# The sums of quarters for Strassen's products: from two engines to one, and lower in the scheduler's order

## The chip, the cores and the metric

The kernel runs on one core of a Trainium2 chip. Its engines work side by side, each through its own list of instructions in order: TensorE (PE) multiplies matrices, VectorE (DVE), ScalarE (ACT) and GpSimd (POOL) work elementwise, and the queue of SyncE (SP) issues the DMA transfers. The metric is the time of one execution in microseconds (us).

## The reference

The reference is two layers of a transformer-like backbone over 512 latent tokens and 256 context tokens of width 1024: a pooling mixer in layer 0, attention in layer 1, and behind each a squared-ReLU MLP with 4096 hidden units.

```
h = h + g1 * mixer(modulate(rms_norm(h)))
m = modulate(rms_norm(h))
h = h + g2 * (square(relu(m @ w1)) @ w2)
```

The change lies in the two MLPs. In layer 0 it also computes the context tokens, in layer 1 the latent tokens alone.

## The kernel before, in words

All activations lie transposed in SBUF: features on the partitions, tokens along the row. To keep float32 precision each operand of a product is split into a high part (ACT copies it, line 84, 379 or 461) and a residual (DVE subtracts, line 85, 381 or 463), and PE makes three products: high by high, high by residual, residual by high. The helper for the split is `hilo`. A weight `w` is thus a DMA into a staging tile `raw` (two buffers, so the DMA for the next one but one waits for the residual to be made), an ACT copy and a DVE subtraction.

An MLP (`mlp`) walks through 16 chunks of 256 hidden units. For each chunk `m1_chunk` (products on line 369) makes `m @ w1` into PSUM; `m1_done` applies ReLU and square (ACT lines 377, 379 and 380, DVE line 381) and leaves `act`. Then `m2_chunk` (products on line 486) makes the product with `w2` for the chunk before, in eight blocks `dt` of 128 output features; after each, DVE adds it to `h_lat` and `h_ctx` (`add_gated`, line 346). The PSUM tiles `mm` have two buffers, `aux` four, so a block waits until an older one has been read.

From chunk 5 of layer 0 and chunk 4 of layer 1 on, the latent part of `m @ w1` is computed by Strassen's scheme: seven products of quarters instead of eight (line 435). For that, five sums or differences of quarters of `m` are prepared once per layer, in `strassen_inputs`. A quarter of `m` is 128 partitions by 1024 numbers, and has a high part and a residual (`m_m_hi`, `m_m_lo`). `total` makes one of them: `s` from the two high parts, on DVE; `e` from the two residuals, on POOL (both line 392); `s + e`, on DVE (line 393); and the split of it by `hilo`. Three of the results are the tiles `xs`; the other two overwrite a quarter of `m` itself. The temporary tiles `s` and `e` are named `op` in layer 0 and `mc` in layer 1.

These five sums are issued in steps beside the first calls of `m2_chunk` (the parameter `side`): in layer 0 from about 132 us on, in layer 1 from about 954 us. In the same stretches DVE also serves the weights and the outputs of the chunks, and in layer 0 the products of layer 1's conditioning vector (`ada1_block`: lines 215 and 217, split into the tiles `ada0` and `ada1`, and PE's products on line 225).

Behind its first part, which is ordered by hand, the order on each engine is made by a list scheduler at build time: among instructions that are ready by its own estimate it takes the one with the lowest rank, and the rank is the place in the program. The order is then fixed: on the chip an engine never overtakes. In the Strassen chunks POOL makes sums of quarters of the weights (line 424, tiles `sc`), with or without this change.

Of the kernel before, what the change touches and what calls it, by code (L numbers as in the profile page):

```python
# [8 lines left out]
F32 = mybir.dt.float32  # L9
F32R = mybir.dt.float32r  # L10
AF = mybir.ActivationFunctionType
ALU = mybir.AluOpType
# [27 lines left out]
ADA_1 = (0, 2, 4, 5, 6, 1, 7, 3, 8, 9, 10, 11)  # L40

STRASSEN_FROM = (5, 4)


@with_exitstack
def dit_block_kernel(ctx: ExitStack, tc: tile.TileContext, xT, cols, adab, adaw, w1, w2, wqkv, wo,
                     poolw, gvec, rope, edge, eye, out):
    nc = tc.nc
    act, dve, pool, pe = nc.scalar, nc.vector, nc.gpsimd, nc.tensor
# [22 lines left out]
    def new(p, shape, dt, tag, bufs=None):  # L72
        uid[0] += 1
        kw = {"bufs": bufs} if bufs else {}
        return p.tile(shape, dt, tag=tag, name=f"{tag}{uid[0]}", **kw)
# [7 lines left out]
    def hilo(hi, lo, src, lo_eng=dve):  # L83
        act.activation(hi, src, AF.Copy)  # L84
        lo_eng.tensor_tensor(lo, src, hi.bitcast(F32), op=ALU.subtract)  # L85
# [297 lines left out]
    def strassen_inputs(m, xs, tmp, cuts):  # L383


        def quarter(i, j):
            return [m[0][x][:, 4 * i : 4 * i + 4, 256 * j : 256 * j + 256] for x in range(2)]

        def total(dst, a, b, op):
            s, e = (new(tmp[0], [P, 4, 256], F32, tmp[1]) for _ in range(2))  # L390
            for o, x, eng in ((s, 0, dve), (e, 1, pool)):
                eng.tensor_tensor(o, a[x].bitcast(F32), b[x].bitcast(F32), op=op)  # L392
            dve.tensor_tensor(s, s, e, op=ALU.add)  # L393
            hilo(dst[0], dst[1], s)

        b11, b12, b21, b22 = (quarter(i, j) for i in range(2) for j in range(2))
        b7, b6, b1 = ([t[:, x] for x in range(2)] for t in xs)
        sums = ((b7, b21, b22, ALU.add), (b6, b11, b12, ALU.add), (b1, b11, b22, ALU.add),
                (b12, b12, b22, ALU.subtract), (b21, b21, b11, ALU.subtract))

        def steps(todo):
            for x in todo:
                total(*x)
                yield
        return (b22, b12, b21, b11, b7, b6, b1), [steps(sums[i:j]) for i, j in zip((0,) + cuts, cuts + (5,))]
# [152 lines left out]
    for g, win in enumerate(WINDOWS):  # L558
# [6 lines left out]
        for e in range(3):  # L565

            todo = [(bands[:, g, e, 1:], cur[:, PAD + 1 : 3 * PAD + P], PAD + 1)]
            if e:
                o = PAD if e == 1 else P
# [12 lines left out]
    for k in range(0, KT, 2):  # L582
        for s, c0, n in segs:
# [4 lines left out]
            dst, src = turned[s][:, : n // P, k * P : k * P + 256], ps.rearrange("p (i c) -> p i c", c=256)  # L588
# [76 lines left out]
    for dt in range(8):  # L665
        if dt % 2 == 0:
            b = (4, 3, 5, 6)[dt // 2]
# [144 lines left out]
    def strassen0(m):  # L812
# [9 lines left out]
        def op():  # L822
# [9 lines left out]
            return tile_of  # L832
        return STRASSEN_FROM[0], strassen_inputs(m, xs, (opp, "op"), (0, 1, 3)), lambda: new(rawp, [P, 2, 1024], F32, "pair"), op

# [238 lines left out]
    def strassen1(m):  # L1073
# [4 lines left out]
        xs = [xsp.tile([P, 2, 4, 256], F32R, tag=f"xs{i}", name=f"xs{i}") for i in range(3)]  # L1078
        return STRASSEN_FROM[1], strassen_inputs(m, xs, (mc, "mc"), (1, 3)), lambda: new(fin, [P, 2, 1024], F32, "fin"), op

# [95 lines left out]
```

## Time and profile before

| | us |
|---|---|
| median of three runs | 1305.57 (1305.48 to 1306.43) |
| the profiled execution | 1306.94 |
| its span, first to last instruction | 1305.2 |
| PE busy in it | 1249.4 |
| DVE busy | 1036.6 |
| ACT busy | 578.4 |
| POOL busy | 325.1 |

The profile shows one execution. A line of its timeline has the start, the length, the engine, the line of the kernel, the operation, the tile written and the tiles read, how many neighbours were merged, and in brackets how long the engine had been idle before it and what ended that. PE's granted clock is 1.00 at 2.4 GHz and 0.50 at 1.2 GHz; a stretch's mean lies between.

### The profile page before, as it was taken

What the parts mean: (1) busy time and instruction counts of PE and PEld (TensorE: products, weight loads), DVE (VectorE), ACT (ScalarE), POOL (GpSimd) and SP (SyncE); (2) the same over time, 40 slices, a digit from 0 to 9 for tenths busy, and PEclk for the clock granted to TensorE, in tenths of its full rate; (3) what the DMA queues carried; (4) which work ended last, traced back from release to release, by engine and by line L of the source; (5) the groups of instructions that cost most, each with busy time, mean ns of one, the idle gap of its engine ahead of it and who ended that gap; (6) DMA issues with size and microseconds to landing.
All of it is one profiled execution on the core that took longest, in us unless ns stands there. A gap on an engine that the chain in (4) does not pass through costs nothing. (4 is left out here: it accounts for less than half of the span.)

```text
span 1305.2 us, 20489 instructions
## 1 busy us (share of the span) xinstructions
PE 1249.4 (96%) x8150; PEld 1109.4 (85%) x8150; DVE 1036.6 (79%) x1671; ACT 578.4 (44%) x954; POOL 325.1 (25%) x223
## 2 busy tenths in 40 slices
PE   7999989999999999999988999999979999999997
PEld 6567868899999999999878799998967899989896
DVE  6564998788989888866888387879899788898976
ACT  5454513444444444443343154445553535444443
POOL 0000320122131322230135122211054244343411
PEclk8999989999999999999999999999989999999998
DMA  9766314333433333301111020111214323322211
GB/s 351 270 241 226 113 54 157 113 130 114 145 109 135 114 129 130 130 33 52 46 57 66 33 66 34 65 33 65 98 33 133 114 95 111 98 97 98 66 33 65
DMA packets 41313, 138.68 MB, mean 106 GB/s; under 512 B 4736, under 2 KB 8064, under 8 KB 41088
## 3 DMA queue, kind: packets, MB, share of 16 engines
q1 hardware_dynamic: 41216, 137.36, 29.9%
q8 instruction: 64, 1.05, 0.3%
q14 instruction: 33, 0.27, 0.1%
HBM read 135.25 MB, written 2.10 MB: 105 GB/s over the span
## 5 line engine op out<-in xcount | busy, mean ns | idle before, releaser
L486 PE MATMUL mm<-act,w 128*128 128x512 f32 (+1 forms) x1224 | 244.4, 352 | 11.9 <-DVE act L381 6.3
L486 PE MATMUL aux<-act,w 128*128 128x512 f32 (+1 forms) x1224 | 240.0, 347 | 3.2 <-DVE h_lat L346 3.1
L486 PEld LDWEIGHTS mm<-act,w 128*128 128x128 f32 x1224 | 199.5, 193 | 44.8 <-DVE act L381 6.6
L486 PEld LDWEIGHTS aux<-act,w 128*128 128x128 f32 x1224 | 196.3, 190 | 32.8 <-DVE h_lat L346 3.9
L84 ACT ACTIVATE w<-raw 128x1024 fp32r<-128x1024 f32 x106 | 110.2, 1054 | 138.2 <-PE aux L486 89.0
L85 DVE TENSOR_TENSOR w<-raw,w 128x1024 fp32r<-128x1024 f32 x87 | 112.4, 1305 | 33.7 <-ACT w L84 33.1
L346 DVE SCALAR_TENSOR_TENSOR h_lat<-aux,mod,h_lat 128x512 f32<-128x512 f32 (+1 forms) x204 | 125.4, 629 | 16.3 <-PE aux L486 14.6
L424 POOL TENSOR_TENSOR sc<-pair 128x512 f32<-128x512 f32 x55 | 76.8, 1405 | 221.4 <-DVE op L430 88.8
L424 POOL TENSOR_TENSOR sc<-fin 128x512 f32<-128x512 f32 x60 | 90.5, 1523 | 154.0 <-DVE r L444 87.4
L346 DVE SCALAR_TENSOR_TENSOR h_lat<-mm,mod,h_lat 128x512 f32<-128x512 f32 (+1 forms) x140 | 96.6, 698 | 7.6 <-PE mm L486 6.7
L369 PE MATMUL mm<-m_m_hi,w 128*128 128x512 f32 (+1 forms) x320 | 92.5, 351 | 1.1 <-ACT m_m_hi L84 1.1
L856 PE MATMUL aux<-w,a_m_hi 128*128 128x256 f32 (+1 forms) x384 | 87.5, 323 | 0.0
L217 DVE SCALAR_TENSOR_TENSOR mc<-raw,s_f,mc 128x512 f32<-128x512 f32 x112 | 84.8, 777 | 2.5 <-DMA raw<-in_dram 1.7
L85 POOL TENSOR_TENSOR w<-raw,w 128x1024 fp32r<-128x1024 f32 x19 | 47.2, 2497 | 100.1 <-ACT w L84 99.7
L435 PE MATMUL mm<-m_m_hi,mc 128*128 128x256 f32 x384 | 71.0, 283 | 0.0
L856 PEld LDWEIGHTS aux<-w,a_m_hi 128*128 128x128 f32 x384 | 64.4, 193 | 4.9
L369 PEld LDWEIGHTS mm<-m_m_hi,w 128*128 128x128 f32 x320 | 56.1, 189 | 11.1 <-ACT m_m_hi L84 1.3
L455 PE MATMUL aux<-m_c,w 128*128 128x256 f32 x528 | 65.2, 283 | 0.0
L455 PEld LDWEIGHTS aux<-m_c,w 128*128 128x128 f32 x528 | 64.2, 192 | 0.0
L463 DVE TENSOR_TENSOR act<-r,act 128x512 fp32r<-128x512 f32 x46 | 48.4, 1052 | 19.8 <-ACT r L462 19.7
L856 PE MATMUL aux<-w,a_m_lo 128*128 128x256 f32 (+1 forms) x192 | 61.7, 321 | 0.0
L435 PEld LDWEIGHTS mm<-m_m_hi,mc 128*128 128x128 f32 x384 | 60.7, 192 | 0.5
(245 smaller groups left out, 2612.1 us busy)
## 6 DMA issues: line engine op xcount, KB each, us to landing
raw<-in_dram SPq DMA_DIRECT2D x157, 512.0 KB, 3.3
praw<-in_dram SPq DMA_DIRECT2D x34, 512.0 KB, 8.1
fin<-in_dram SPq DMA_DIRECT2D x24, 512.0 KB, 4.1
pair<-in_dram SPq DMA_DIRECT2D x22, 512.0 KB, 4.2
block<-in_dram SPq DMA_DIRECT2D x8, 512.0 KB, 6.2
h_lat<-in_dram SPq DMA_DIRECT2D x4, 512.0 KB, 6.4
w<-in_dram SPq DMA_DIRECT2D x4, 512.0 KB, 10.7
out_dram<-fin SPq DMA_DIRECT2D x8, 256.0 KB, 2.5
```

The costliest lines, as they stand in the source:

```text
L84: act.activation(hi, src, AF.Copy)
L85: lo_eng.tensor_tensor(lo, src, hi.bitcast(F32), op=ALU.subtract)
L217: dve.scalar_tensor_tensor(acc[:, s], w, scal, acc[:, s], op0=ALU.mult, op1=ALU.add)
L346: dve.scalar_tensor_tensor(h, ps, gate[:, dt, s : s + 1], h, op0=ALU.mult, op1=ALU.add)
L369: pe.matmul(ps[:, c0 : c0 + cn], lhs, ms(m, ax, k, c0, cn), start=k + wx + ax == 0, stop=k == KT - 1 and wx == 1)
L424: pool.tensor_tensor(t, x, y, op=how)
L435: pe.matmul(places[n], w[:, wx, k * P : k * P + P], inputs[n][ax][:, k], start=k + wx + ax == 0, stop=k == 3 and wx == 1)
L455: pe.matmul(pc[:, t * 256 : t * 256 + 256], ws[k // 4][:, wx, k % 4 * P : k % 4 * P + P], ms(m, ax, k, SEQ, CTX), start=k + wx + ax == 0, ...
L463: dve.tensor_tensor(lo, r, hi.bitcast(F32), op=ALU.subtract)
L486: pe.matmul(ps, lhs, a[:, t, ax, c0 : c0 + n], start=t + wx + ax == 0, stop=t == 1 and wx == 1)
L856: pe.matmul(ps, lhs, ws[u][:, wx, o : o + width], start=k + ax + wx == 0, stop=k == KT - 1 and ax == 1)
```

## The change

In `total`, the sum of the residuals `e` is made by DVE instead of POOL, and everything that `total` issues (three DVE sums, ACT's copy and DVE's residual) is issued under `tc.high_priority(offset=-600)`: its rank in the scheduler is 600 places later than where it stands in the program, so that other ready work is taken first.

```
+BEHIND = 600
...
         def total(dst, a, b, op):
             s, e = (new(tmp[0], [P, 4, 256], F32, tmp[1]) for _ in range(2))
-            for o, x, eng in ((s, 0, dve), (e, 1, pool)):
-                eng.tensor_tensor(o, a[x].bitcast(F32), b[x].bitcast(F32), op=op)
-            dve.tensor_tensor(s, s, e, op=ALU.add)
-            hilo(dst[0], dst[1], s)
+
+            with tc.high_priority(offset=-BEHIND):
+                for o, x in ((s, 0), (e, 1)):
+                    dve.tensor_tensor(o, a[x].bitcast(F32), b[x].bitcast(F32), op=op)
+                dve.tensor_tensor(s, s, e, op=ALU.add)
+                hilo(dst[0], dst[1], s)
```

Ten instructions leave POOL and ten come to DVE, five for each layer. The order changes in two stretches alone, around the sums of either layer. Line numbers of the changed kernel are higher by 2, or by 4 behind `total`.

The first place is DVE in layer 0, from the residual of the weight `w232` on. Tiles `op` are `s` and `e` of three sums, `xs00` and `xs01` their results, `act219` the output of a chunk's `m1_done`, `w232`, `w234` and `w257` weights. Before:

```order
L85 TENSOR_TENSOR w232_1476<-raw233_1477,w232_1476 128x1024
L392 TENSOR_TENSOR op236_1486<-m_m_hi_713 128x1024
L85 TENSOR_TENSOR ada1_1198<-mc202_1196,ada0_1197 128x512
L393 TENSOR_TENSOR op236_1486<-op236_1486,op237_1487 128x1024
L85 TENSOR_TENSOR w234_1481<-raw235_1482,w234_1481 128x1024
L392 TENSOR_TENSOR op273_1796<-m_m_hi_713 128x1024
L85 TENSOR_TENSOR xs00_1193<-op236_1486,xs00_1193 128x1024
L393 TENSOR_TENSOR op273_1796<-op273_1796,op274_1797 128x1024
L392 TENSOR_TENSOR op276_1818<-m_m_hi_713 128x1024
L85 TENSOR_TENSOR w257_1644<-raw258_1645,w257_1644 128x1024
L85 TENSOR_TENSOR xs01_1194<-op273_1796,xs01_1194 128x1024
L381 TENSOR_TENSOR act219_1333<-r225_1393,act219_1333 128x768
```

And now, in the same place:

```order
L87 TENSOR_TENSOR w232_1476<-raw233_1477,w232_1476 128x1024
L87 TENSOR_TENSOR ada1_1198<-mc202_1196,ada0_1197 128x512
L396 TENSOR_TENSOR op236_1486<-m_m_hi_713 128x1024
L396 TENSOR_TENSOR op237_1487<-m_m_lo_714 128x1024
L87 TENSOR_TENSOR w234_1481<-raw235_1482,w234_1481 128x1024
L397 TENSOR_TENSOR op236_1486<-op236_1486,op237_1487 128x1024
L396 TENSOR_TENSOR op273_1796<-m_m_hi_713 128x1024
L396 TENSOR_TENSOR op274_1797<-m_m_lo_714 128x1024
L87 TENSOR_TENSOR xs00_1193<-op236_1486,xs00_1193 128x1024
L87 TENSOR_TENSOR w257_1644<-raw258_1645,w257_1644 128x1024
L383 TENSOR_TENSOR act219_1333<-r225_1393,act219_1333 128x768
L397 TENSOR_TENSOR op273_1796<-op273_1796,op274_1797 128x1024
```

The sums of the residuals (`op237`, `op274`) have come in, and `w257` and `act219` now stand ahead of the second sum's last step instead of behind it.

The second place is ACT in layer 0, behind the first half of a chunk's ReLU (`r225`); `r227` is the second half, read from `mm226`. Before:

```order
L377 ACTIVATE r225_1393<-mm224_1344 128x768
L84 ACTIVATE w257_1644<-raw258_1645 128x1024
L379 ACTIVATE act219_1333<-r225_1393 128x768
L84 ACTIVATE xs01_1194<-op273_1796 128x1024
L380 ACTIVATE r225_1393<-r225_1393 128x768
L84 ACTIVATE xs02_1195<-op276_1818 128x1024
L377 ACTIVATE r227_1447<-mm226_1398 128x768
L84 ACTIVATE w259_1649<-raw260_1650 128x1024
```

And now:

```order
L379 ACTIVATE r225_1393<-mm224_1344 128x768
L86 ACTIVATE w257_1644<-raw258_1645 128x1024
L381 ACTIVATE act219_1333<-r225_1393 128x768
L382 ACTIVATE r225_1393<-r225_1393 128x768
L86 ACTIVATE xs01_1194<-op273_1796 128x1024
L379 ACTIVATE r227_1447<-mm226_1398 128x768
L86 ACTIVATE w259_1649<-raw260_1650 128x1024
L381 ACTIVATE act219_1333<-r227_1447 128x768
```

The copy into `xs02` stood ahead of the ReLU `r227`; it has left this stretch and stands six instructions behind it.

The third place is DVE in layer 1, from the end of the norm on. `mc1454` and `mc1477` are `s` of the first two sums, `act1434` the first chunk's output, `w1450` and `w1452` the weights of the first `m2_chunk`, `mm1456` its first block. Before:

```order
L85 TENSOR_TENSOR m2_m_lo_9378<-sc1433_9601,m2_m_hi_9377 128x2x256
L392 TENSOR_TENSOR mc1454_9866<-m2_m_hi_9377 128x1024
L392 TENSOR_TENSOR mc1477_10018<-m2_m_hi_9377 128x1024
L85 TENSOR_TENSOR w1450_9856<-raw1451_9857,w1450_9856 128x1024
L393 TENSOR_TENSOR mc1454_9866<-mc1454_9866,mc1455_9867 128x1024
L393 TENSOR_TENSOR mc1477_10018<-mc1477_10018,mc1478_10019 128x1024
L392 TENSOR_TENSOR mc1480_10033<-m2_m_hi_9377 128x1024
L381 TENSOR_TENSOR act1434_9617<-r1446_9833,act1434_9617 128x512
L381 TENSOR_TENSOR act1434_9617<-r1447_9838,act1434_9617 128x512
L85 TENSOR_TENSOR w1452_9861<-raw1453_9862,w1452_9861 128x1024
L85 TENSOR_TENSOR xs0_9853<-mc1454_9866,xs0_9853 128x1024
L346 SCALAR_TENSOR_TENSOR h_lat_98<-mm1456_9873,mod1_135,h_lat_98 128x512
```

And now, from the first sum's second instruction on:

```order
L396 TENSOR_TENSOR mc1455_9867<-m2_m_lo_9378 128x1024
L87 TENSOR_TENSOR w1450_9856<-raw1451_9857,w1450_9856 128x1024
L87 TENSOR_TENSOR h_ctx1516_10259<-sc1528_10344,h_ctx1516_10259 128x512
L397 TENSOR_TENSOR mc1454_9866<-mc1454_9866,mc1455_9867 128x1024
L396 TENSOR_TENSOR mc1477_10018<-m2_m_hi_9377 128x1024
L396 TENSOR_TENSOR mc1478_10019<-m2_m_lo_9378 128x1024
L383 TENSOR_TENSOR act1434_9617<-r1446_9833,act1434_9617 128x512
L383 TENSOR_TENSOR act1434_9617<-r1447_9838,act1434_9617 128x512
L87 TENSOR_TENSOR w1452_9861<-raw1453_9862,w1452_9861 128x1024
L87 TENSOR_TENSOR w1465_9938<-raw1466_9939,w1465_9938 128x1024
L348 SCALAR_TENSOR_TENSOR h_lat_98<-mm1456_9873,mod1_135,h_lat_98 128x512
```

Ahead of `act1434` one last step and one first step of a sum have gone, and two sums of residuals and an operand of a Strassen product (`h_ctx1516`, half as long) have come.

## Rows read from the trace of the kernel before

**Rows 1.** The page's first lines: span, then busy time, share and instructions by engine.

```profile
span 1305.2 us, 20489 instructions
PE 1249.4 (96%) x8150; PEld 1109.4 (85%) x8150; DVE 1036.6 (79%) x1671; ACT 578.4 (44%) x954; POOL 325.1 (25%) x223
```

**Rows 2.** PE's waits over the whole span: releaser, us in total, times, longest.

```profile
PE mm L486 <- DVE act L381: 6.3, 1, 6.3
...
PE mm L486 <- ACT r L377: 3.0, 1, 3.0
...
PE mm L486 <- DVE h_lat L346: 2.3, 1, 2.3
...
PE aux L225 <- DVE ada L85: 1.9, 1, 1.9
```

**Rows 3.** Timeline of PE in layer 0: start, length, work, count, idle before.

```profile
141.69 4.32 PE L486 MATMUL aux<-act,w 128*128 128x512 f32 x24
...
162.49 2.24 PE L486 MATMUL mm<-act,w 128*128 128x512 f32 x12
167.78 3.56 PE L486 MATMUL mm<-act,w 128*128 128x512 f32 x12 [3.05 <-ACT r L377]
...
188.18 0.51 PE L369 MATMUL mm<-m_m_hi,w 128*128 128x512 f32 x1
```

**Rows 4.** Windows in layer 0: busy time of each engine, then granted clock, DMA.

```profile
168.00:172.00 4.00, 4.00 (x15) 3.43 (x15) 4.00 (x4) 2.25 (x3) 1.32 (x1) 0.57 0.00 0
```

**Rows 5.** Timeline of ACT in layer 0.

```profile
165.97 1.06 ACT L84 ACTIVATE xs<-op 128x1024 fp32r<-128x1024 f32 x1 [5.83 <-DVE op L393]
```

**Rows 6.** Timeline of DVE in layer 0.

```profile
147.28 1.21 DVE L85 TENSOR_TENSOR w<-raw,w 128x1024 fp32r<-128x1024 f32 x1
148.41 1.21 DVE L392 TENSOR_TENSOR op<-m_m_hi 128x1024 f32<-128x1024 f32 x1
...
159.36 3.44 DVE L85 TENSOR_TENSOR w<-raw,w 128x1024 fp32r<-128x1024 f32 x1
...
163.86 0.95 DVE L381 TENSOR_TENSOR act<-r,act 128x768 fp32r<-128x768 f32 x1
164.72 1.21 DVE L393 TENSOR_TENSOR op<-op,op 128x1024 f32<-128x1024 f32 x1
```

**Rows 7.** Timeline of POOL, one sum in layer 0 and one in layer 1.

```profile
158.39 3.32 POOL L392 TENSOR_TENSOR op<-m_m_lo 128x1024 f32<-128x1024 f32 x1 [1.34 <-DVE op L393]
...
985.26 10.73 POOL L392 TENSOR_TENSOR mc<-m_m_lo 128x1024 f32<-128x1024 f32 x1 [10.38 <-DVE xs L85]
```

**Rows 8.** Timeline of PE in layer 1.

```profile
962.87 0.39 PE L486 MATMUL mm<-act,w 128*128 128x512 f32 x1
969.59 4.89 PE L486 MATMUL mm<-act,w 128*128 128x512 f32 x11 [6.33 <-DVE act L381]
...
993.37 2.88 PE L486 MATMUL mm<-act,w 128*128 128x512 f32 x12
996.09 2.88 PE L486 MATMUL aux<-act,w 128*128 128x512 f32 x12
...
1002.68 1.66 PE L486 MATMUL mm<-act,w 128*128 128x512 f32 x6 [2.35 <-DVE h_lat L346]
...
1006.90 0.39 PE L369 MATMUL mm<-m_m_hi,w 128*128 128x512 f32 x1
```

**Rows 9.** Timeline of DVE in layer 1.

```profile
954.36 4.56 DVE L392 TENSOR_TENSOR mc<-m_m_hi 128x1024 f32<-128x1024 f32 x2
...
961.08 4.57 DVE L393 TENSOR_TENSOR mc<-mc,mc 128x1024 f32<-128x1024 f32 x2
965.58 3.35 DVE L392 TENSOR_TENSOR mc<-m_m_hi 128x1024 f32<-128x1024 f32 x1
968.86 1.28 DVE L381 TENSOR_TENSOR act<-r,act 128x512 fp32r<-128x512 f32 x2
```

**Rows 10.** DMA issues: tile, queue, count, size, median us to landing.

```profile
raw<-in_dram SPq DMA_DIRECT2D x157, 512.0 KB, 3.3
```

## The prediction

> **What bounds the kernel now.** I read the page first: PE is busy for 1249.4 of 1305.2 us [rows 1], so what counts is where PE stands still or runs at its lower clock. The waits of PE come next. Of its few, four lie in the two stretches in which the sums are made: 6.3, 3.0, 2.3 and 1.9 us [rows 2]. The reader is to see in the timeline that each has the sums behind it.
>
> In layer 0 PE finishes a block at 164.73 and needs the PSUM tile that ACT's second ReLU reads [rows 3]. ACT is held in front of that ReLU by the copy into `xs`, for which it idled 5.83 us until DVE's last step of a sum, at 164.72 [rows 5, 6]. DVE is late because one weight residual took 3.44 us instead of the 1.13 from one start to the next that such rows have; POOL's sum started at 158.39 and ran across it [rows 6, 7]. After the gap the granted clock is 0.57 in one window of 4 us, between 1.2 and 2.4 GHz [rows 4].
>
> In layer 1 PE starts the first `m2_chunk` at 962.87, makes one product and waits 6.33 us for the residual of `act`, made at 968.86 on DVE [rows 8, 9]. Ahead of it DVE spent 4.56, 4.57 and 3.35 us on five instructions of the sums, 12.5 us in place of 5.7 [rows 9]. Then eleven products take 4.89 us where twelve take 2.88 [rows 8]: the lower clock again.
>
> **What there is to win.** From 164.73 to 188.18 are 23.45 us [rows 3]. Between them lie 72 products of `m2_chunk` (three times the 24 that took 4.32, so 13.0) and 12 small ones of the conditioning, which I set at the mean of those 24, 0.18 each, so 2.2 (an estimate). The excess is 8.3 us: 5.0 of waits [rows 2], the rest clock and short gaps. From 962.87 to 1006.90 are 44.0 us, with 144 products 512 wide; twelve take 2.72 from 993.37 to 996.09 [rows 8], so they need 32.6. The excess is 11.4 us. Together 19.7 us can be won at most, since elsewhere the order stays.
>
> **The price of the edit on DVE.** Ten additions more, of a shape that the trace shows: 1.13 us each, 5.7 per layer. POOL's ten go. What their going gives DVE lies between nothing and the 2.3 us that the row at 159.36 lost; I take 2.2 for those that meet DVE, since the three rows of layer 1 lost 6.8 us (12.5 - 5.7) in one hold each [rows 9], the same size. So DVE gives 1.13 and gets about 2.2 where it met POOL and loses 1.13 where it did not.
>
> The row at 985.26 speaks against: there POOL needed 10.73 us [rows 7], because DVE went on with its own additions and kept POOL out. The Trainium skill (SBUF — State Buffer, Who interferes with whom) says that of a GpSimd operation and a DVE operation with two SBUF inputs the one that starts first has the shared ports for its whole length and the other is blocked. By that rule a sum met by a DVE that is already running costs DVE nothing, and its move costs 1.13 us. Both orders occur in the trace, as the two rows of POOL show, and were the second the usual one the time would be that of the third rival below.
>
> **Layer 0, step by step.** I go through the new order on DVE with these pitches, from 147.28 [rows 6]: `w232` to 148.4, `ada1` (half as long, 0.6 as the 512 wide pair in 1.28 [rows 9]) to 149.0, two sums to 151.3, `w234` to 152.4, the last step to 153.6, two sums to 155.8, the residuals of `xs00` and `w257` to 158.1, `act219` (0.86, from 163.86 to 164.72 [rows 6]) to 159.0, the second sum's last step to 160.1 instead of 165.9. ACT's copy into `xs01` (1.06 [rows 5]) ends at 161.2. The copy into `xs02` has moved behind the ReLU, so ACT is free when the first products end at 162.49, and the ReLU, under 0.85 us (PE went on 1.81 us after the start of a copy that took 1.06 [rows 3, 5]), is done by 163.5. PE asks at 164.73. The wait of 3.05 goes with 1.2 us to spare, and with it the drop of the clock.
>
> Next is the conditioning's residual, for which PE waited 1.9 us [rows 2]. On DVE it comes 18 instructions and some waits for PE after 160.1; with the same pitches I find its end near 173.8 and PE at its product near 174.4. Its high part is tighter, since PE asks for it two products after the row that ACT's copy waits for: 0.4 us may stay. What is late after that? The two weights of the next `m2_chunk`, whose DMA waits for the staging tile that DVE's conditioning products read. These run some 8 us earlier too, because PE's transposes ahead of them do; with 3.3 us from issue to landing [rows 10], an ACT copy and the DVE queue (with two of the yielding sums now between the two weights, 2.3 us) I have the last residual at 200.1 and PE asking at 200.9. I leave 0.3 for it. Layer 0 keeps 8.3 - 0.4 - 0.3 = 7.6 us.
>
> **Layer 1, step by step.** DVE from 954.36: two sums, of which one meets POOL's sum of weights (+1.2, half the hold above, as it is half as long), to 957.9; `w1450`, for which ACT now first waits for POOL, to 959.6; `h_ctx` 0.6; then last step, sum, sum, of which one meets POOL's next (+1.2), to 964.8; the residual of `act` to 965.4, instead of 969.5. PE asks at 963.1 and waits 2.3. Then `w1452`, one `act` further, ends at 967.1, and PE's first block needs it 0.5 us sooner. In all 3 us of the 6.33 stay, with an uncertainty of 1 us either way from who goes first. A wait of 2.35 left the clock up in this trace (six products in 1.66 behind it [rows 8]) and that of 3.05 took it down, so I set half of the clock's loss (about 2 us, eleven products in 4.89 instead of 2.7), 0.9, as staying. The later wait of 2.35 [rows 8] was for an output addition of DVE behind POOL's 10.73; in the new order, by the same pitches, that addition ends 1.8 us before PE asks for its tile. So layer 1 keeps 11.4 - 3.0 - 0.9 = 7.5 us.
>
> The remaining sums are late but not too late: the last overwrites its quarter of `m` near 1017, and the Strassen product that reads it comes near 1023. POOL's gain is worth nothing by itself.
>
> **The sum.** 7.6 + 7.5 = 15.1 us. The profiled execution took 1306.94 (span 1305.2 and 1.74 around it), 1.37 above the median of 1305.57; I take the gain from the median: 1290.5.
>
> **The rivals.**
> Only layer 0 gains. In layer 1 ACT's copy of `w1450` now stands behind a copy that waits for POOL, and POOL can be kept out for long [rows 7]; the waits of 6.3 and 2.3 then stay about as they are. 1305.6 - 7.6 = 1298.0, with half of the later wait gone 1297, with a tight weight in layer 0 up to 1303. For it: that queue on ACT; against: DVE itself waits for the same copy, so POOL gets in within 2 us.
>
> No change, 1303 to 1308 (within 0.2%, 2.6 us, which is about what a measurement can tell here). PE would come 8 us early to stretches that DVE or the weights' DMA set, and give it back. Against it: the view of PE's waits lists none at all from 190 to 625, so PE sets the pace there.
>
> Slower. DVE is full in both stretches, and the 3.44 and 4.56 are not POOL's doing, or POOL is mostly the one kept out. Then 5.7 us come onto the chain behind which PE waits, in each layer: 1305.6 + 11.4 = 1317. It decides once the lengthened rows stay above 2 us in the new trace. Against it: POOL's rows lie over each of them.
>
> **How the numbers follow.** Forecast 64%, own range 1285 (nearly all of 19.7) to 1297. Only layer 0 18%, no change 9%, slower 9%. So faster 0.82, same 0.09, slower 0.09. The range leaves out the last two and a little of the first: 1285 to 1302.
>
> **What would show it.** Right: PE's waits for ACT's ReLU near 167 and for `ada` near 181 are gone and the clock stays 1.00 there; the wait at 963 is 2 to 4 us and the one at 1000 gone; all 30 additions of the sums at 1.2 us on DVE, none of the weight residuals between 147 and 200 above 2 us; POOL 10 instructions fewer, DVE 10 more but busy for no more than before. Wrong: additions of the sums that take 2 to 3 us; a wait of PE for `w` near 200 or for a quarter of `m` near 1020; a new wait of more than 1 us between 200 and 620.

## The result, and the profile after

The changed kernel takes 1291.3 us (median of four runs, 1290.52 to 1293.01), the kernel before in the same runs 1306.0: a ratio of 0.9881, 95% interval 0.9855 to 0.9907. The forecast was 1290.5. Two later comparisons of the same kernel gave 1289.11 (0.9870, 0.9852 to 0.9888) and 1290.14 (0.9881, 0.9864 to 0.9898), so its gain lies between 14.7 and 17.5 us.

The page's first lines of the profile after, to be set beside [rows 1]:

```profile
span 1291.2 us, 20478 instructions
PE 1247.2 (97%) x8150; PEld 1107.8 (86%) x8150; DVE 1031.4 (80%) x1681; ACT 578.4 (45%) x954; POOL 292.0 (23%) x213
```

DVE has ten instructions more and is busy for 5.2 us less. Ten additions at 1.13 are 11.3 us, so the ten sums that left POOL had cost DVE 16.5 us, 1.65 each.

Of PE's four waits [rows 2] one is left in the list of waits after:

```profile
PE mm L490 <- DVE act L383: 0.6, 1, 0.6
```

PE in layer 0, timeline of after, answering to [rows 3], and the window that answers to [rows 4]:

```profile
163.61 4.40 PE L490 MATMUL mm<-act,w 128*128 128x512 f32 x24
167.85 4.40 PE L490 MATMUL aux<-act,w 128*128 128x512 f32 x24
172.09 0.63 PE L227 MATMUL aux<-ada,ones 128*128 128x512 f32 x2
...
175.07 0.39 PE L227 MATMUL aux<-ada,ones 128*128 128x512 f32 x1
...
180.21 0.50 PE L371 MATMUL mm<-m_m_hi,w 128*128 128x512 f32 x1
```

```profile
168.00:172.00 4.00, 4.00 (x25) 3.44 (x24) 3.75 (x8) 0.00 (x0) 0.00 (x0) 1.00 0.34 125
```

24 products stand together where a gap of 3.05 us was, and the granted clock is 1.00 (2.4 GHz) where it was 0.57. The reason is on ACT and DVE, here the timelines that answer to [rows 5, 6]:

```profile
160.86 1.06 ACT L86 ACTIVATE xs<-op 128x1024 fp32r<-128x1024 f32 x1 [2.16 <-DVE op L397]
163.81 0.81 ACT L379 ACTIVATE r<-mm 128x768 f32<-128x768 f32 x1 [1.89 <-PE mm L371]
```

```profile
147.86 1.21 DVE L87 TENSOR_TENSOR w<-raw,w 128x1024 fp32r<-128x1024 f32 x1
...
157.54 1.22 DVE L87 TENSOR_TENSOR w<-raw,w 128x1024 fp32r<-128x1024 f32 x1
158.74 0.96 DVE L383 TENSOR_TENSOR act<-r,act 128x768 fp32r<-128x768 f32 x1
159.61 1.22 DVE L397 TENSOR_TENSOR op<-op,op 128x1024 f32<-128x1024 f32 x1
```

The weight residual takes 1.22 us and not 3.44, and ACT's ReLU at 163.81 now waits for PE, not for a sum. In layer 1, PE and then DVE, answering to [rows 8, 9]:

```profile
959.08 0.39 PE L490 MATMUL mm<-act,w 128*128 128x512 f32 x1
960.06 1.19 PE L490 MATMUL mm<-act,w 128*128 128x512 f32 x4 [0.59 <-DVE act L383]
...
993.16 0.39 PE L371 MATMUL mm<-m_m_hi,w 128*128 128x512 f32 x1
```

```profile
950.21 2.29 DVE L396 TENSOR_TENSOR mc<-m_m_lo 128x1024 f32<-128x1024 f32 x1
...
955.95 2.32 DVE L396 TENSOR_TENSOR mc<-m_m_hi 128x1024 f32<-128x1024 f32 x1
958.20 1.21 DVE L396 TENSOR_TENSOR mc<-m_m_lo 128x1024 f32<-128x1024 f32 x1
959.33 1.28 DVE L383 TENSOR_TENSOR act<-r,act 128x512 fp32r<-128x512 f32 x2
```

Of the 30 instructions of the sums these two at 2.3 us are the only long ones. POOL's sums of weights, started at 949.23 and 955.04, lie beside them.

For the comparison of profiles three stretches of PE are enough. Layer 0's: from the first product of `m1_chunk` near 146 (145.85 before, 146.65 after) to the next such block (188.18 and 180.21). Layer 1's: from the end of PE's last short wait for `m_m_lo`, ahead of the first `m2_chunk` (954.49, 949.21), to the `m1_chunk` at 1006.90 and 993.16. The attention's: from the last products of weights in layer 0 (609.43, 601.25) to that same short wait. In us, each from one profile. The variants are described in the next section; "the yield" is the rank of 600 places later, "DVE alone" is the change without it:

| kernel | layer 0 | attention | layer 1 |
|---|---|---|---|
| before | 42.3 | 345.1 | 52.4 |
| changed | 33.6 | 348.0 | 44.0 |
| changed, second and third profile | 33.6, 33.6 | 344.7, 347.7 | 44.0, 44.0 |
| DVE alone, two profiles | 33.5, 33.6 | 346.5, 343.3 | 42.8, 42.6 |
| yield alone | 39.3 | 343.4 | 53.3 |
| change in layer 1 only | 40.8 | 344.9 | 44.0 |
| change in layer 0 only | 33.5 | 348.1 | 52.7 |
| POOL's sums beside, unread | 40.0 | 346.1 | 52.7 |
| yield of 100 | 33.5 | 346.1 | 42.6 |

Layer 0 wins 8.8 us and layer 1 8.4 us, 17.2 together. The 42.3 of layer 0 is the one profile of before: the same instructions in the same order took 40.8 us in the run with the change in layer 1 only, where PE had the full clock behind its wait of 1.5 us for `ada` (twelve products in 2.28 us, in the profile of before 3.62 behind 1.9). Against that one layer 0 wins 7.2 us. The attention, of which the change touches nothing, takes 343 to 348 us, and for one kernel it differs by 3 us between profiles.

### The profile page after: what moved, and what is told of

The parts are those of the page before. It is cut to its first block, busy times and chain, and to the rows that moved or that the text cites. A ratio compares the mean times of both kernels' runs of the same rounds, so it can differ in the third digit from the quotient of the medians.

```text
span 1291.2 us, 20478 instructions
## 1 busy us (share of the span) xinstructions
PE 1247.2 (97%) x8150; PEld 1107.8 (86%) x8150; DVE 1031.4 (80%) x1681; ACT 578.4 (45%) x954; POOL 292.0 (23%) x213
## 5 line engine op out<-in xcount | busy, mean ns | idle before, releaser
L490 PE MATMUL mm<-act,w 128*128 128x512 f32 (+1 forms) x1224 | 239.2, 347 | 0.6 <-DVE act L383 0.6
L490 PEld LDWEIGHTS mm<-act,w 128*128 128x128 f32 x1224 | 196.2, 190 | 32.1 <-issue 1.7
L348 DVE SCALAR_TENSOR_TENSOR h_lat<-aux,mod,h_lat 128x512 f32<-128x512 f32 (+1 forms) x204 | 125.4, 628 | 16.5 <-PE aux L490 14.6
L428 POOL TENSOR_TENSOR sc<-fin 128x512 f32<-128x512 f32 x60 | 96.2, 1619 | 172.7 <-DVE r L448 83.6
L87 DVE TENSOR_TENSOR w<-raw,w 128x1024 fp32r<-128x1024 f32 x87 | 108.0, 1256 | 27.9 <-ACT w L86 27.5
L371 PEld LDWEIGHTS mm<-m_m_hi,w 128*128 128x128 f32 x320 | 57.4, 194 | 11.2 <-ACT m_m_hi L86 1.2
```

Of the source, the lines that this page charges most:

```text
L348: dve.scalar_tensor_tensor(h, ps, gate[:, dt, s : s + 1], h, op0=ALU.mult, op1=ALU.add)
L371: pe.matmul(ps[:, c0 : c0 + cn], lhs, ms(m, ax, k, c0, cn), start=k + wx + ax == 0, stop=k == KT - 1 and wx == 1)
L428: pool.tensor_tensor(t, x, y, op=how)
L490: pe.matmul(ps, lhs, a[:, t, ax, c0 : c0 + n], start=t + wx + ax == 0, stop=t == 1 and wx == 1)
```

## The experiments

Two theories. **Contention**: a sum on POOL with both inputs in SBUF holds DVE's instructions of the same kind (they take longer while it runs), and that is what made PE late. **Order**: the yield lets the weights' residuals, `act` and the ReLU go ahead of the sums. A variant of the first is that not the contention but the wait of DVE's last step for POOL's end was the price.

**DVE alone.** The kernel before, without the yield:

```
-            for o, x, eng in ((s, 0, dve), (e, 1, pool)):
+            for o, x, eng in ((s, 0, dve), (e, 1, dve)):
```

> The kernel before with one word changed: the second half-sum of each sum of quarters on DVE, at its old place in the scheduler's eyes (no yielding). Hold theory (GpSimd's half-sums hold DVE's instructions and make its last steps wait): DVE's ten half-sums and five last steps run at about 1.2 us each, the waits of TensorE near 167 and 181 us and the one near 963 us go, and the time falls by most of the 14.7 us that the change brought: 1291 to 1294 us. Order theory (the yield puts the sums behind the weights' residuals, and the copies of the sums behind ScalarE's ReLU): with no yield the sums still stand ahead of what TensorE asks for, each 3.6 us of DVE, so the waits near 167 and 963 us stay at 2 us or more each, and the time is 1300 to 1306 us.

Measured: 1289.76 us, ratio 0.9868 (0.9847 to 0.9889). The whole gain is there, as contention has it, even a little more than its 1291 to 1294. No wait for the sums is left near 167, 181 or 963; of the 30 instructions one took 2.29 us, the others 1.2. Order as the cause falls.

**Yield alone.** The changed kernel with the second half-sum back on POOL:

```
-                for o, x in ((s, 0), (e, 1)):
-                    dve.tensor_tensor(o, a[x].bitcast(F32), b[x].bitcast(F32), op=op)
+                for o, x, eng in ((s, 0, dve), (e, 1, pool)):
+                    eng.tensor_tensor(o, a[x].bitcast(F32), b[x].bitcast(F32), op=op)
```

> The changed kernel with the second half-sum of each sum of quarters back on GpSimd, and the yield kept. Hold theory: DVE's instructions beside GpSimd's half-sums still take 2.3 to 3.5 us instead of 1.2, GpSimd's own 3 to 10 us, and the last steps still wait for GpSimd: the time stays at 1302 to 1306 us. Order theory: the weights' residuals and the ReLU residual come first, TensorE's waits near 167 and 963 us go, and the time is 1291 to 1296 us; the held DVE instructions are then only late sums that nobody waits for.

Measured: 1305.41 us, ratio 0.9995 (0.9983 to 1.0008): nothing is gained. In this profile layer 0 is 3.0 us shorter than in that of before and layer 1 0.9 us longer. PE's waits, then DVE, then POOL in layer 0:

```profile
PE mm L490 <- DVE act L383: 8.0, 1, 8.0
...
PE mm L490 <- ACT r L379: 6.5, 3, 3.3
```

```profile
157.99 1.22 DVE L87 TENSOR_TENSOR w<-raw,w 128x1024 fp32r<-128x1024 f32 x1
159.12 3.42 DVE L396 TENSOR_TENSOR op<-m_m_hi 128x1024 f32<-128x1024 f32 x1
162.47 0.95 DVE L383 TENSOR_TENSOR act<-r,act 128x768 fp32r<-128x768 f32 x1
163.34 1.21 DVE L87 TENSOR_TENSOR xs<-op,xs 128x1024 fp32r<-128x1024 f32 x1
164.47 1.21 DVE L397 TENSOR_TENSOR op<-op,op 128x1024 f32<-128x1024 f32 x1
```

```profile
158.15 3.31 POOL L396 TENSOR_TENSOR op<-m_m_lo 128x1024 f32<-128x1024 f32 x1 [2.47 <-DVE xs L87]
```

The weight residual is now ahead of POOL's sum and takes 1.22 us; the next instruction takes the hold in its place, 3.42 us for 1.13, and the last step ends at 165.7 as before. The yield changes who is held, not that somebody is.

**One layer at a time.** The changed lines for `mc` alone (layer 1), or for `op` alone (layer 0), the old ones for the other:

```
+            new_way = tmp[1] == "mc"
+            with tc.high_priority(offset=-BEHIND) if new_way else ExitStack():
+                for o, x, eng in ((s, 0, dve), (e, 1, dve if new_way else pool)):
```

> The change in the sums of layer 1 alone; layer 0's sums are made as before. If the two layers' gains stand beside each other and nothing links them, layer 0 keeps its 8 us of waits and half clock, and layer 1 gives back what it did in the changed kernel, 44.0 to 34.1 us from its first product to its last, less the 1.5 us of half clock just ahead of it: 8.4 us, so 1297 us (1296 to 1298.5). If the half clock at 950 us and the 2.9 us that the changed kernel gave back in the attention between 609 and 949 us come of layer 0 being early, they are not here, TensorE is level with the kernel before until 949 us, and the time is nearer 1295.5 us. If layer 0's gain was the whole of it, 1306 us.

> The change in the sums of layer 0 alone; layer 1's sums are made as before. If the layers' gains stand beside each other and what layer 0 wins is kept, 8.8 us less: 1297 us. If part of it is given back in the attention in any run (the changed kernel's lead fell from 8.1 us at 609 us to 5.2 us at 949 us, by lower granted clock and one longer wait, where no instruction was changed), 1299.5 to 1301 us, with the same low clock near 660 to 680 us. If the low clock there differs from run to run, the lead at 949 us in this profile is anywhere from 5 to 8 us. Layer 1 shows the old waits of 6.3 and 2.3 us either way.

Measured: layer 1 alone 1296.16 us, ratio 0.9920 (0.9902 to 0.9939), 10.1 us under before; layer 0 alone 1298.69, 0.9935 (0.9919 to 0.9952), 7.6 us under. The two add up to 17.7, against 14.7 to 17.5 for both at once: the gains stand beside each other. The second lies between its two expectations. Its waits in layer 1 are 4.8, 1.1 and 0.7 us and not 6.3 and 2.3, but the stretch is as long as before (52.7). Layer 0's profile had a slow attention (348.1) and the half clock ahead of layer 1; layer 1's had neither. At this point I took that for an effect of the early layer 0, since three profiles with it had the half clock and three without had not.

**POOL's sums beside, unread.** DVE does all the work in three steps, and POOL makes the old sum into a tile that nothing reads:

```
+                dve.tensor_tensor(s, a[0].bitcast(F32), b[0].bitcast(F32), op=op)
+                pool.tensor_tensor(e, a[1].bitcast(F32), b[1].bitcast(F32), op=op)
+                dve.tensor_tensor(s, s, a[1].bitcast(F32), op=ALU.add)
+                dve.tensor_tensor(s, s, b[1].bitcast(F32), op=op)
```

> The changed kernel, with GpSimd's ten half-sums made beside it for nobody: DVE adds the four quarters one after another in three steps of its own (as many instructions as in the changed kernel), and GpSimd sums the same two quarters as in the kernel before into a tile that nothing reads. This leaves the contention and takes the dependency away. If contention is the price, DVE's steps that meet GpSimd's take 2.3 to 3.4 us again instead of 1.2, about 2.2 us for each of the ten sums met, TensorE's waits near 167 us (ReLU) and near 957 us (ReLU residual) come back, and the time is 1299 to 1306 us. If the price was the wait of DVE's last step for GpSimd's end, DVE never waits here, held steps are few, and the time is 1290 to 1294 us.

Measured: 1309.08 us, ratio to before 1.0014 (1.0004 to 1.0025), 20 us above the changed kernel in the same runs (1289.11) and more than the 1299 to 1306 that contention was given. Both stretches are about as long as before (40.0 and 52.7). The wait for `act` is back; the one for the ReLU near 167 is not, instead PE waits 4.9 us near 177 for an addition to `h_lat`. PE's waits, and DVE and POOL in layer 1:

```profile
PE mm L490 <- DVE act L383: 5.9, 1, 5.9
...
PE aux L227 <- DVE h_lat L348: 4.9, 1, 4.9
```

```profile
953.26 3.45 DVE L394 TENSOR_TENSOR mc<-m_m_hi 128x1024 f32<-128x1024 f32 x2
957.27 2.79 DVE L87 TENSOR_TENSOR w<-raw,w 128x1024 fp32r<-128x1024 f32 x1 [0.57 <-ACT w L86]
959.99 2.89 DVE L87 TENSOR_TENSOR h_ctx<-sc,h_ctx 128x512 fp32r<-128x512 f32 x1
962.81 3.42 DVE L396 TENSOR_TENSOR mc<-mc,m_m_lo 128x1024 f32<-128x1024 f32 x2
...
967.28 1.28 DVE L383 TENSOR_TENSOR act<-r,act 128x512 fp32r<-128x512 f32 x2
```

```profile
955.59 6.75 POOL L395 TENSOR_TENSOR mc<-m_m_lo 128x1024 f32<-128x1024 f32 x2
963.03 2.11 POOL L428 TENSOR_TENSOR sc<-fin 128x512 f32<-128x512 f32 x1 [0.70 <-DVE h_ctx L87]
```

The list of DVE's waits has none for POOL's sums here, and DVE has the same 1681 instructions as in the changed kernel. It is busy for 1052.7 us instead of 1031.4: 2.1 us for each of the ten sums. The order on DVE is not quite that of the changed kernel, and no run has it without POOL's sums; but in layer 1 seven instructions of the same sizes stand ahead of `act` in both, and from the first of them to `act` DVE needs 14.0 us here (953.26 to 967.28) and 10.3 in the changed kernel (949.08 to 959.33). So contention alone is enough for the price, and waits for POOL's end are not needed for it. The kernel before had two of these besides, 2.3 us each, one in either layer:

```profile
157.08 1.23 DVE L393 TENSOR_TENSOR op<-op,op 128x1024 f32<-128x1024 f32 x1 [2.31 <-POOL op L392]
```

What share of the loss they had there, no run tells apart.

**A smaller yield.** `BEHIND` 600 to 100.

> The changed kernel with the yield cut from 600 to 100. With no yield at all the kernel with DVE alone took 1289.8 us, with 600 it took 1291.3, and with the yield but GpSimd's half-sums 1305.4. If the yield is worth nothing, this is 1288 to 1292 us, no different from either. If the yield of 600 costs 1.5 us in layer 1, where it puts ScalarE's and DVE's copies of the sums late, a smaller one gives 1289 to 1290 us.

Measured: 1289.28 us, ratio 0.9864 (0.9846 to 0.9881).

**The changed kernel and DVE alone once more, side by side.** No edit.

> The changed kernel once more, beside the next one on one chip, for two things: its time against the kernel with DVE alone and no yield, and whether the half clock in the attention between 609 and 949 us, and the one just ahead of layer 1's first products, belong to the kernel or to a run. If they belong to the kernel, this profile has them at the same instructions (0.7 and 0.85 some 32 and 28 us ahead of TensorE's third short wait near 949 us, and half clock for 3.5 us behind that wait), 9.87 us from that wait to the first product; if to a run, they are elsewhere or missing, 8.4 us there. The time is 1291 us either way, 1290 to 1293.

> DVE alone without the yield, once more, beside the changed kernel on one chip. If the yield costs or brings nothing, the two agree within 0.1% (1 us or so, 1289 to 1292 us here). If the yield costs, this one is again 1 to 2 us the faster: 1289 to 1290 us. Its clock shows the same half clock at the same instructions if that belongs to the early layer 0, 346 to 348 us from the last weight products of layer 0 to the third short wait near 944 us.

Measured: 1289.11 us (0.9870, 0.9852 to 0.9888) with the yield, a little below the range expected, and 1289.72 (0.9869, 0.9851 to 0.9887) without. The yield of 600, that of 100 and none are the same to what these runs can tell: without it layer 1's stretch is 1.3 us shorter, but from its end to the end of the span it takes 300.0 us and not 298 to 298.4, with a wait of 1.13 us for ScalarE near 998.

The half clock is not the kernel's. Windows of the changed kernel's first profile, then of the second:

```profile
660.00:680.00 20.00, 16.77 (x66) 13.44 (x65) 16.00 (x30) 6.75 (x13) 8.02 (x7) 0.83 0.15 53
...
940.00:960.00 20.00, 16.82 (x120) 15.90 (x119) 19.11 (x21) 11.22 (x18) 8.52 (x5) 0.91 0.08 27
```

```profile
660.00:680.00 20.00, 16.82 (x80) 13.65 (x79) 17.71 (x35) 8.26 (x15) 6.30 (x7) 1.00 0.15 53
...
940.00:960.00 20.00, 16.06 (x105) 14.12 (x106) 19.12 (x19) 12.76 (x21) 7.34 (x5) 1.00 0.17 55
```

Same kernel, 0.83 and 0.91 in one, 1.00 in the other. My reading of the one-layer profiles, that the early layer 0 brings it, was wrong.

**The weights' sums too.** If contention is the price, POOL's other sums cost as well. DVE alone, with this besides:

```
-                pool.tensor_tensor(t, x, y, op=how)
+                dve.tensor_tensor(t, x, y, op=how)
```

> DVE alone without the yield, and GpSimd's 115 sums of weight blocks (128x512, 1.29 us each where nothing is beside them, 170 us in all) moved to DVE as well. If every GpSimd sum beside a DVE sum costs DVE about what it takes there, moving all of them frees DVE again and the time falls below 1289 us, by 1 to 4 us, since the two half-sums still held to 2.3 us near 945 and 990 us go. If it matters only where TensorE stands behind DVE in the same stretch, nothing is won in the stretches of Strassen's products (TensorE waits for nothing of GpSimd or of these sums there), DVE has 115 more instructions of some 0.65 us, about 75 us less what it is no longer held, and the time is 1289 to 1292 us, or longer, 1293 to 1300, if DVE at 80% busy now comes late in Strassen's last steps.

Measured: 1285.05 us, ratio 0.9834 (0.9814 to 0.9855). Again, beside the changed kernel:

> The kernel with the half-sums and the sums of weights on DVE once more, on one chip with the changed kernel below. In the first profile TensorE's three short waits ahead of layer 1's products (1.04, 0.8 and 0.8 us), the two behind the first product (0.40 and 0.55) and the one for ScalarE near 998 us (1.13) were gone, 4.7 us in all: if that is the gain, this is 3 to 5 us below the changed kernel in the same runs, about 1285 us. If the 1285.05 was the luck of one chip, the two agree within 1 us.

> The changed kernel for the third time, as the other half of the comparison above: 1289 to 1291.5 us. Its half clock stretches between 609 and 953 us differ again from those of the two profiles before, if they belong to the run: 343 to 348 us from the last weight products of layer 0 to the third short wait.

Measured: 1285.07 (0.9845, 0.9829 to 0.9861) against 1290.14 (0.9881, 0.9864 to 0.9898): this version beats both kernels, the changed one by 5.1 us. Its sums by line, on DVE; the second group is the same sums on POOL, in the second profile of DVE alone:

```profile
L424 DVE TENSOR_TENSOR sc<-fin x60: 676/681/686, 943.2 to 1238.8; 128x512 f32<-128x512 f32 x60
L424 DVE TENSOR_TENSOR sc<-pair x55: 677/683/687, 242.6 to 583.4; 128x512 f32<-128x512 f32 x55
```

```profile
L424 POOL TENSOR_TENSOR sc<-fin x60: 1282/1614/3407, 935.9 to 1227.6; 128x512 f32<-128x512 f32 x60
L424 POOL TENSOR_TENSOR sc<-pair x55: 1276/1297/1747, 177.6 to 577.6; 128x512 f32<-128x512 f32 x55
```

115 sums of 0.68 us are 78 us more for DVE, or 69 at the 0.60 from one start to the next that such rows have in a run of them; but it is busy for 1052.9 us and not 1033.3, so 50 to 59 us come back in holds that are gone. Of PE's waits in the kernel with DVE alone, the three short ones ahead of layer 1 (1.04, 0.8 and 0.8 us), the 0.40 and 0.55 behind its first product and the 1.13 near 998 are gone from the list, 4.7 us.

## Why the prediction was right, point by point

**DVE's price** (give 1.13, get about 2.2 for a sum met) was right: 2.1 where all ten sums were put beside DVE, 1.65 in the mean over those of the kernel before, of which some were kept out by DVE [rows 7]. The rule of the Trainium skill (SBUF — State Buffer, Who interferes with whom), that whoever starts first has the ports, agrees with rows such as the 3.42 us above. In the row of 10.73 POOL was kept out not by one instruction of DVE but by the seven that followed one another from 986.23 on, each at its usual length (1.22 us, the half as long one 0.69), and of such a run the rule says nothing. It tells no price without the count of who came first, and here POOL came first often enough.

**Layer 0**, step by step, less the 0.8 us by which this profile comes later: the second sum's last step ends at 160.0 (160.1 forecast), ACT's copy at 161.1 (161.2), the ReLU at 163.8 (163.5), while PE asks for the tile near 165.0 (half of the 24 products behind 163.61), 1.2 us later, as forecast. The conditioning's residual ends at 173.8 (173.8), with PE at its product at 174.3 (174.4). The two amounts I left as lost, 0.4 for its high part and 0.3 for the last weight, did not occur: PE waits for neither. 8.8 us were won and 7.6 forecast; beside these two amounts, the twelve small products of the conditioning took 1.6 us and not the 2.2 I had set. Against the other profile of the old layer 0 (40.8) it is 7.2, so that the sum for this layer agrees as well as these runs can tell.

**Layer 1.** The wait of 2.3 for `act`: 2.11 in the second profile; 0.59 in the first, where PE had come 1.5 us later by its half clock just ahead. Both give 44.0 us, since DVE sets the end there, so that loss of clock costs nothing. The further 0.5 for the second weight was no wait of PE. Behind the wait the 47 products took 11.2 us (960.06 to 971.23) and not 10.7 as at 2.72 for twelve, half of the 0.9 I had set for the clock. The wait of 2.35 near 1000 is gone. 8.4 us were won and 7.5 forecast. The wait in the second profile:

```profile
955.01 1.19 PE L490 MATMUL mm<-act,w 128*128 128x512 f32 x4 [2.11 <-DVE act L383]
```

**The sum** was too low by 2.1 us for the two stretches, and had no term for what the clock does elsewhere, which moves a run by more than that: the attention alone took 348.0, 344.7 and 347.7 us in three profiles of the changed kernel, 345.1 in that of before. In the first comparison the two nearly cancelled (14.7 against 15.1), in the second they did not (17.5): that the first came within 0.4 us of the forecast gain was in part luck.

**The rivals.** "Only layer 0" fell with the run of layer 1 alone; ACT's copy behind POOL cost DVE 0.56 us (953.07, idle before the weight) and no more. "Slower" would have needed long additions in the new trace. One line of my list was careless: it wanted all 30 additions at 1.2 us, though the working had two that meet POOL's sums of weights, and these took 2.3. The list of waits has nothing new above 1 us between 200 and 620.

That the change's second half, the yield, is worth nothing was not forecast; I had put the order's moves into the steps without asking which half of the change they needed.

## What to carry to other kernels

An elementwise instruction on GpSimd with its inputs in SBUF isn't free help when VectorE is working beside it: in this kernel each 128x1024 sum cost VectorE 1.65 us in the mean and 2.1 where all ten lay beside it, against 1.13 for making it there. Look for VectorE rows at two or three times their usual length and see what lies beside them on GpSimd, and count what VectorE gets back before calling it full. To tell contention from waiting, leave the helper's work in and its reader out.

## What the runs showed of the hardware

VectorE's output additions, which read one operand from PSUM, are not held. In the trace of the kernel before, DVE, then POOL:

```profile
166.99 2.61 DVE L215 TENSOR_SCALAR mc<-raw,s_f 128x512 f32<-128x512 f32 x1
...
178.94 0.47 DVE L346 SCALAR_TENSOR_TENSOR h_ctx<-aux,mod,h_ctx 128x256 f32<-128x256 f32 x1
179.33 2.02 DVE L85 TENSOR_TENSOR ada<-mc,ada 128x512 fp32r<-128x512 f32 x1
```

```profile
166.02 3.30 POOL L392 TENSOR_TENSOR op<-m_m_lo 128x1024 f32<-128x1024 f32 x1 [4.30 <-DVE op L393]
178.44 2.37 POOL L392 TENSOR_TENSOR op<-m_m_lo 128x1024 f32<-128x1024 f32 x1 [9.12 <-DVE op L393]
```

The addition to `h_ctx` starts inside POOL's second sum and keeps its 0.47 us; of the 488 additions of line 346 none took more than 0.75. The residual behind it, with both inputs in SBUF, takes 2.02 us for 0.68 and ends 0.5 us behind POOL's end. The Trainium skill (SBUF — State Buffer, Who interferes with whom) states this difference, between two SBUF inputs and at most one outside VectorE's 2-port modes, and the rows agree. One input in SBUF is not always free: the TENSOR_SCALAR at 166.99, with one tensor to read, takes 2.61 us beside POOL's first sum, where the median of the sixteen on its line is 0.48. Whether it ran in such a mode no row shows.

The granted clock of one kernel differs from run to run behind the same gaps. From the end of the short wait ahead of layer 1 to its first product PE took 8.4 us in seven of the table's eleven profiles, with the clock at 1.00, and 9.9 us in the other four, with a stretch at half clock, and the same three waits (1.04, 0.8 and 0.8 us) ahead in all. The changed kernel is on either side. All four are of kernels whose layer 0 is early, four of seven such profiles and none of the other four, which is too few to tell. What decides it these runs do not show.
